# Joint of output projection and feed-forward: a fetch ahead of a large store, weight sums ahead of an input sum, the last rows' steps moved up

## The chip, the cores and the metric

One core of a Trainium2 chip runs the whole program in one launch. The metric is device time in microseconds (us). TensorE (PE) multiplies matrices, VectorE (DVE), ScalarE (ACT) and GpSimd (POOL) work element by element, and SyncE (SP) issues every DMA of this kernel. Each engine takes its instructions in the order in which they were built; waits between engines go over semaphores.

## The reference

One layer of a hybrid decoder on 2048 prompt tokens and 64 sample tokens, 1024 wide, in float32. After attention and gated linear attention, which this change leaves alone, the layer ends so:

```python
mix = jnp.einsum('bte,ed->btd', jnp.concatenate([attn.astype(x.dtype), gla_out], axis=-1), w_out)
x = x + rms_norm(mix, g_mix_post)

h = rms_norm(x, g_ffn_pre)
u = jax.nn.relu(jnp.einsum('btd,df->btf', h, w_up))     # w_up (1024, 4096)
f = jnp.einsum('btf,fd->btd', u * u, w_down)            # w_down (4096, 1024)
x = x + rms_norm(f, g_ffn_post)
```

## The kernel before

**Numbers.** An operand is split into a high and a low part (ACT copies the rounded high part, DVE subtracts it to get the low part), and a product of two operands is three passes on PE. `split_by` makes one such split, `split_in_place` does it for a tile that holds the raw values in the place of its low part.

**Stages.** The rows are worked off in tiles of 128 tokens, 16 of the prompt and one (number 16) of the samples. The output projection takes them in the order `B_ORDER`, which ends with 14, 11, 15. Behind each projection, `residual(i, ...)` does the row work: squares and their sums on ACT, the power -0.5 on POOL, the normalization and the residual sum on DVE (tiles `x1`, `bx`), a second normalization, transposes on PE (`xnT`), and copies into a tile `ht`. The feed-forward then works on two blocks of 1024 tokens (`sb` 0 and 1) and 16 slices of 256 features (`fc`), with a seven-product scheme in place of eight: the input is needed as seven combinations `H[1]` to `H[7]`, the weights as `w` (quarters), `s13` and `s24` (sums of quarters, made in a tile `t13` and split). Four subtractions turn the four quarters in `ht` into the seven combinations, which are stored to `h_d` in DRAM (1,792 KB for each pair of row tiles) and fetched back as `hraw_*`, or, for `H[3]` and `H[4]`, into the place of their low part. `residual` is a generator: each `next(last_rows)` in the code runs the last row tile (15) up to the next `yield`.

**The joint.** While PE does the first slice (`fc` = 0 of `sb` = 0), the last row tiles are finished between its products. The products come in the order `UP_FIRST` = 1, 0, 2, 8, 5, 7, 9, 6, 3, 4; 1 to 7 are products of twelve matmuls, 0, 8 and 9 are steps for the sample tokens (`sam`). `opening(p, ...)` lists what the other engines do behind each. Products 1 and 2 go to the same PSUM bank `ub`: product 1's result is copied out first (`st<-ub` on ACT), then product 2 is added on top of it in the bank. So PE's product 2 waits for that copy. In the trace, products 1 and 2 write `ub`, 5 and 3 write `uc`, 7 and 4 `ud`, 6 `ua`; the next slice begins with `ua` (product 1), `uc` (product 5) and `ue` (product 7).

**Order.** `te`, `ac` and `dv` are PE, ACT and DVE with their instructions held in the order of the code; most instructions of the joint (line L129) are issued so. Other instructions are placed by a scheduler, which also decides when memory of a released pool is taken up again. A tile put where another was waits for the last reader of the other. The output of the up stage is stored slice by slice (`s_d`), and the down stage begins by fetching its first operands (`rs` from `s_d`, `rt` from `t_d`), splitting them into `o0s`, `o1s`, `o0t`, `o1t` and multiplying (`dn`).

Of the kernel before, what the change touches and what calls it, by code (L numbers as in the profile page):

```python
# [16 lines left out]
ALU = mybir.AluOpType  # L17
# [33 lines left out]
DOWN_ORDER = (6, 1, 5, 3, 2, 7, 4)  # L51
DOWN_SUMS = (3, 5, 7, 9, 11, 13)
H_FETCH = ((6, 6), (1, 0), (1, 8), (5, 0), (5, 8), (3, 0), (3, 8))
H_EARLY, H_LATE = (1, 2), (5, 7, 6, 4, 3)
G_EARLY, G_LATE = (0, 1), (2, 3)
A_FILL = ((11, 2, 0), (10, 0, 2), (10, 0, 0), (12, 1, 0))
A_LEAD, A_SPLIT = 14, (2, 1, 0, 0)
# [82 lines left out]
def hybrid_step_kernel(ctx: ExitStack, tc: tile.TileContext, I, O):  # L140
    nc = tc.nc
# [1219 lines left out]
    early = []  # L1361
# [68 lines left out]
    def residual(i, banks, tensor=nc.tensor, scalar=nc.scalar, vector=nc.vector):  # L1430

        n = rows(i)
        x = res_x.pop(i, None) or load_x(i)[0]
        ssq = sp.tile([P, 48], F32, tag="ssq", name=f"bssq_{i}", bufs=2)
        junk = sp.tile([P, D], mybir.dt.bfloat16, tag="junk", name=f"bjunk_{i}", bufs=1)
        x1 = R["x"].tile([P, D], F32, tag="x1", name=f"x1_{i}", bufs=2)
        if i == NB:
            banks = [folded(x1[:NS, c * 512 : (c + 1) * 512], p_) for c, p_ in enumerate(banks)]
        if banks:
            yield from mixed(i, banks, x, x1, junk, ssq, gpost, sp, scalar, vector)  # L1440
        rs = ssq[:, 3:5]
        scalar.activation(junk[:n], x[:n], AF.Square, accum_out=ssq[:n, 2:3])
        yield
        rsqrt_mean(sp, rs[:n, 1:2], ssq[:n, 2:3], n, D, vector=vector)
        vector.scalar_tensor_tensor(x1[:n], x[:n], rs[:n, 1:2], gpre[:n], op0=ALU.mult, op1=ALU.mult)
        yield
        sb, j, second = i // 8, i % 4, i % 8 >= 4
        q = slice(j * P, (j + 1) * P)
        if i < NB and not second and i:
            sums[sb, j] = ht_place(f"ht_{i}")  # L1450
        for h in range(2):
            kk = slice(h * 4, h * 4 + 4)
            pt = (bank([P, 512], "ce"[h], f"xnT_{i}_{h}") if te is tensor else next_bank("cdce", f"xnT_{i}_{h}")).rearrange("p (k t) -> p k t", k=4)
            for k in range(4):
                tensor.transpose(pt[:, k, :n], x1[:n, (h * 4 + k) * P : (h * 4 + k + 1) * P], ident[:n, :n])
            if i == NB:
                split_copy(xsT[:, kk, :NS], xsT[:, kk, NS:], pt[:, :, :NS], vector)
                continue
            ht = sums[sb, j]
            scalar.activation(ht[:, (6, 2)[h] if second else h], pt, AF.Copy)  # L1460
            if sb == 0 and not second:
                split_copy(H[h + 1][0][:, :, q], H[h + 1][1][:, :, q], pt, vector)
        if i == NB or not second:
            return
        yield
        for out, a, b in ((4, 6, 0), (6, 2, 6), (5, 2, 4), (3, 1, 5)):
            vector.tensor_tensor(ht[:, out], ht[:, a], ht[:, b], op=ALU.subtract)
        kept = slice(2 * (sb == 0), 7)
        nc.sync.dma_start(h_d[sb][:, kept, :, q], ht[:, kept])

    h_raws = {}

    def fetch_h(sb, p, home="h"):
        h_raws[p] = []
        for k in range(0, KT // 2, 2):
            if isinstance(home, tuple):
                pool, tag = U[home[k // 2]], "s"
            else:
                pool, tag = {"h": hs_pool, "t": keep}.get(home) or U[home], f"{home}{k // 2}"
            raw = pool.tile([P, 2, BT], F32, tag=tag, name=f"hraw_{sb}_{p}_{k}", bufs=1)  # L1480
            nc.sync.dma_start(raw, h_d[sb][:, p - 1, k : k + 2])
            h_raws[p].append(raw)

    def load_h(sb, p, scalar=nc.scalar, vector=nc.vector):
        h_place(sb, p)
# [38 lines left out]
    for n, i in enumerate(B_ORDER[2:]):  # L1524
        early.append((i, []))
        mixing = out_projecting(nc.tensor, i, early[-1][1])
        run(mixing, 24 if i == B_ORDER[-1] else 48)
        if n == 0:
            second = residual(*early.pop(1))
            next(second)  # L1530
            next(second)
        elif n == 1:
            run(second)
        if n != 1:
            run(residual(*early.pop(0)))
        run(mixing)
        if n == len(B_ORDER) - 5:
            load_up(0, 0)
            split_up(0, 0, 0)
            split_up(0, 0, 1)  # L1540
            fetch_h(0, 5)
# [6 lines left out]
        h_pools[p] = open_pool(f"h_{p}", "right")  # L1548
    U["tmp"] = open_pool("u0_tmp", "right")
    fetch_h(0, 7, ("s24h", "s24l"))  # L1550
    fetch_h(0, 6, "tmp")


    def quarters(sb, fc):
# [9 lines left out]
    def sums_24(sb, fc, vector):  # L1564

        (a11, a21), (a12, a22) = quarters(sb, fc)
        t = sums[sb, fc]
        vector.tensor_tensor(t[:, :, 0], t[:, :, 0], a11, op=ALU.subtract)
        vector.tensor_tensor(t[:, :, 1], a12, t[:, :, 0], op=ALU.subtract)

    def split_sums(sb, fc, n, scalar, vector):
        halves_[sb, fc, n] = parts = [
            U[f"s{n}{'hl'[u]}"].tile([P, KT // 2, 2, P], F32R, tag="s", name=f"s{n}{u}_{sb}_{fc}", bufs=1) for u in range(2)
        ]
        split_by(scalar, vector, *parts, sums[sb, fc])
# [150 lines left out]
    def opening(p, taken, ahead):  # L1726

        if p == 1:
            taken(p)
        elif p == 0:  # L1730
            next(last_rows)
        elif p == 2:
            taken(p)
            next(last_rows)
            run(load_h(0, 6, ac, dv))
            U.pop("tmp").release()
        elif p == 8:
            taken(p)
            sums_24(0, 0, dv)
            split_sums(0, 0, 24, ac, dv)  # L1740
        elif p == 5:
            taken(p)
        elif p == 7:
            taken(p)
            next(last_rows)
            close_pools(R)
            for q in H_LATE[3:]:
                h_pools[q] = open_pool(f"h_{q}")
            for q in H_LATE[:2:-1]:
                h_place(0, q)  # L1750
                for k in range(0, KT // 2, 2):
                    loaded = nc.sync.dma_start(f32(H[q][1][:, k : k + 2]), h_d[0][:, q - 1, k : k + 2])
            with tc.issue_after(loaded.ins):
                load_up(0, 2)
        elif p == 9:
            taken(p)
        elif p == 6:
            split_in_place(3)
            ahead("a")
            taken(p)  # L1760
            split_in_place(4)
            run(last_rows)
            for half in range(2):
                load_down(0, half)
        elif p == 3:
            ahead("s13")
            ahead("13")
        else:
            ahead("s24")
            ahead("24")  # L1770
# [268 lines left out]
    sums_13(0, 0, dv)  # L2039
    run(load_h(0, 5, ac, dv))  # L2040
    split_sums(0, 0, 13, ac, dv)
    load_up(0, 1)
    next(last_rows)
    run(load_h(0, 7, ac, dv))
    for sb in range(NSB):
# [11 lines left out]
            run(ends)  # L2057
        deque(end, 0)
        if sb == 0:
            for p in (3, 4, 7, 6):  # L2060
                h_pools.pop(p).release()
        close_pools(U)
        if sb == 0:
# [53 lines left out]
```

## Time and profile before

| | |
|---|---|
| median of 3 runs | 2221.18 us (2219.98 to 2222.38) |
| profiled execution, own time | 2222.0 us |
| its span, first to last instruction | 2220.2 us |
| mean granted clock of PE in it | 0.996 |
| busy, share of the span | PE 98%, PEld 84%, DVE 68%, ACT 55%, POOL 12% |
| share of the 16 DMA engines (hardware queue) | 55.7% |
| last projection matmuls of row tile 15 | about 901.5 us from the span's start |
| first slice of the up stage on PE | 902.25 to 933.84 us |
| start of the down stage of block 0 | 1258.00 us |

A timeline row has the start in us, the length in us, the engine, the source line, the operation, output<-input, shapes and count; in brackets stands how long the engine was idle before it, and what ended that. Rows that follow each other in one group are merged. In a row of the windows view stand, for each engine, the busy time and the number of instructions in that stretch, then PE's granted clock, the share of the DMA engines and GB/s. Matmul ends are modelled and overlap the next start.

### The profile page before, as it was taken

Reading aid. Unit: us, or ns where it says so; the run is one execution under the profiler, and the core shown is the slowest. Engines: PE = TensorE matmul, PEld = TensorE weight load, DVE = VectorE, ACT = ScalarE, POOL = GpSimd, SP = SyncE. Lnnn points to the kernel's source line nnn. Section 1 sums busy time; section 2 is a strip of 40 time slices with the busy share of each in tenths; the row PEclk is TensorE's granted clock in tenths of the full one; section 3 lists DMA queues with packets and bytes.
Section 4 is the critical chain, followed back from the end, with each engine's and each line's share of the span. In section 5 each row is a group of like instructions: output and inputs, shape, how many; then the busy total and the mean of one; then the engine's idle time right before and its main releaser. Section 6 shows DMA issues by size and latency. Waiting matters only on the chain.

```text
span 2220.2 us, 34144 instructions
## 1 busy us (share of the span) xinstructions
PE 2172.9 (98%) x11784; PEld 1863.6 (84%) x11784; DVE 1518.6 (68%) x3101; ACT 1218.7 (55%) x2626; POOL 261.7 (12%) x417
## 2 busy tenths in 40 slices
PE   8999999999999999899999999999999999999998
PEld 7889888999998888688888887888888888888886
DVE  5888777777876665788888655547776666555566
ACT  6788866556664443555555554435454545444444
POOL 3566522111111100000000000000000000000000
PEclk9999999999999999999999999999999999999999
DMA  7344322214436665867877677767553444666685
GB/s 236 121 137 146 104 90 84 67 58 132 152 110 230 205 194 192 256 218 256 277 272 244 242 238 233 235 192 259 186 186 140 148 157 147 227 199 196 194 267 188
DMA packets 240010, 411.53 MB, mean 185 GB/s; under 512 B 25877, under 2 KB 142077, under 8 KB 235725
## 3 DMA queue, kind: packets, MB, share of 16 engines
q1 hardware_dynamic: 239836, 409.35, 55.7%
q8 instruction: 93, 1.52, 0.3%
q14 instruction: 81, 0.66, 0.1%
HBM read 266.34 MB, written 143.98 MB: 185 GB/s over the span
## 4 chain that ended last, share of the span: by engine, by line
PE 77%; DVE 9%; ACT 8%; DMA 3%; issue 2%; POOL 1%; SPq 0%; DVEq 0%; ACTq 0%; POOLq 0%
PE dn L129 25%; PE gproj L129 9%; PE uc L129 7%; PE ua L129 7%; PE out L1269 6%; PE ud L129 4%; PE ub L129 4%; PE ue L129 4%; ACT s L129 2%; PE proj L129 2%; PE sam L129 1%; PE dsam L129 1%; DVE s L129 1%; PE o L129 1%; PE xT L129 1%
## 5 line engine op out<-in xcount | busy, mean ns | idle before, releaser
L129 PE MATMUL dn<-o0t,o0s 128*128 128x512 f32 x896 | 349.3, 390 | 2.4 <-ACT f L1891 1.1
L129 PE MATMUL dn<-o1t,o0s 128*128 128x512 f32 x896 | 349.5, 390 | 0.5 <-DVE o1t L217 0.5
L129 PE MATMUL dn<-o0t,o1s 128*128 128x512 f32 x896 | 349.3, 390 | 0.0
L217 DVE TENSOR_TENSOR o1s<-rs,o0s 128x512 fp32r<-128x512 f32 x224 | 154.8, 691 | 231.2 <-ACT o0s L216 228.4
L216 ACT ACTIVATE o0s<-rs 128x512 fp32r<-128x512 f32 x224 | 141.1, 631 | 305.8 <-PE dn L129 283.8
L129 PE MATMUL gproj<-wg,gx 128*128 128x384 f32 x1408 | 264.7, 342 | 2.9 <-ACT dec L1025 1.8
L129 PEld LDWEIGHTS gproj<-wg,gx 128*128 128x128 f32 x1408 | 241.0, 188 | 7.8 <-issue 3.9
L129 ACT ACTIVATE st<-st 128x512 f32<-128x512 f32 x224 | 141.2, 630 | 141.9 <-DVE st L129 137.9
L129 PEld LDWEIGHTS dn<-o0t,o0s 128*128 128x128 f32 x896 | 168.2, 188 | 39.9 <-ACT f L1891 1.5
L129 PEld LDWEIGHTS dn<-o1t,o0s 128*128 128x128 f32 x896 | 168.2, 188 | 37.4 <-DVE o1t L217 1.4
L129 PEld LDWEIGHTS dn<-o0t,o1s 128*128 128x128 f32 x896 | 168.2, 188 | 35.2
L129 PE MATMUL uc<-H,s 128*128 128x512 f32 x768 | 187.7, 393 | 1.7 <-ACT s L129 1.2
L129 PE MATMUL ua<-H,w 128*128 128x512 f32 x744 | 179.2, 390 | 0.0
L129 PEld LDWEIGHTS uc<-H,s 128*128 128x128 f32 x768 | 143.6, 189 | 33.2 <-ACT s L129 1.6
L129 PEld LDWEIGHTS ua<-H,w 128*128 128x128 f32 x744 | 139.7, 188 | 29.4
L1269 PE MATMUL out<-wo,mt 128*128 128x512 f32 x680 | 158.6, 392 | 0.0
L217 DVE TENSOR_TENSOR o1t<-rt,o0t 128x512 fp32r<-128x512 f32 x224 | 153.5, 685 | 7.5 <-ACT o0t L216 7.3
L206 POOL TENSOR_TENSOR frs<-rs_v,half 128x1 f32<-128x1 f32 (+1 forms) x13 | 10.1, 787 | 1214.7 <-DVE rs_v L204 693.5
L1269 PEld LDWEIGHTS out<-wo,mt 128*128 128x128 f32 x680 | 126.5, 188 | 26.1
L216 ACT ACTIVATE o0t<-rt 128x512 fp32r<-128x512 f32 x224 | 138.2, 617 | 8.5 <-DMA rt<-t_d 8.2
L129 DVE TENSOR_TENSOR st<-st 128x512 f32<-128x512 f32 x160 | 110.6, 691 | 26.6 <-ACT st L129 22.3
L129 ACT ACTIVATE s<-t 128x1024 fp32r<-128x1024 f32 x62 | 65.7, 1060 | 96.8 <-PE ua L129 27.9
(393 smaller groups left out, 4224.8 us busy)
## 6 DMA issues: line engine op xcount, KB each, us to landing
s_d<-st SPq DMA_DIRECT2D x32, 1792.0 KB, 9.8
rs<-s_d SPq DMA_DIRECT2D x224, 256.0 KB, 2.9
raw<-in_w_up SPq DMA_DIRECT2D x64, 512.0 KB, 4.6
rt<-t_d SPq DMA_DIRECT2D x128, 256.0 KB, 4.4
rt<-in_w_down SPq DMA_DIRECT2D x96, 256.0 KB, 3.2
t<-in_w_down SPq DMA_DIRECT2D x64, 256.0 KB, 4.1
t_d<-t SPq DMA_DIRECT2D x32, 512.0 KB, 3.4
gx<-xt_d SPq DMA_DIRECT2D x28, 512.0 KB, 6.0
```

The lines of the kernel that those rows point to most:

```text
L129: ins = call(*a, **k)
L206: nc.gpsimd.tensor_tensor(out, v[:n], e, op=ALU.pow)
L216: nc.scalar.activation(hi, src, AF.Copy)
L217: vector.tensor_tensor(lo, src, f32(hi), op=ALU.subtract)
L1269: te.matmul(banks[c], x, w[:, c * 512 : (c + 1) * 512], start=k + u == 0, stop=k == KT - 1 and u == len(products) - 1,)
```

## The change

- The store of row tiles 10 and 14 to `h_d` is held back by one `yield`, until both fetches of `H[6]` have been issued; the load of the second slice of `w_up` now comes behind that store as well.
- For row tile 15, the residual sum and the second square are now issued before the splits of `H[7]` and before product 1's copy; the second normalization goes behind sample step 0, and the transposes behind product 5 instead of product 7.
- The weight sums `s24` (`sums_24`) go behind step 0 and their split ahead of the splits of `H[6]`.
- The four subtractions of the last `ht` go from DVE to POOL.
- `H[3]` and `H[4]` swap their places in memory and their order of loading; the loads come behind product 5 and no longer behind product 7, and with them the loads of a third slice of `w_up` and of the first pieces of `w_down`. `H[3]`'s split comes behind step 9, ahead of the split of the next `w`.

```diff
--- before.py
+++ after.py
@@ -51,7 +51,7 @@
 DOWN_ORDER = (6, 1, 5, 3, 2, 7, 4)
 DOWN_SUMS = (3, 5, 7, 9, 11, 13)
 H_FETCH = ((6, 6), (1, 0), (1, 8), (5, 0), (5, 8), (3, 0), (3, 8))
-H_EARLY, H_LATE = (1, 2), (5, 7, 6, 4, 3)
+H_EARLY, H_LATE = (1, 2), (5, 7, 6, 3, 4)
 G_EARLY, G_LATE = (0, 1), (2, 3)
 A_FILL = ((11, 2, 0), (10, 0, 2), (10, 0, 0), (12, 1, 0))
 A_LEAD, A_SPLIT = 14, (2, 1, 0, 0)
@@ -1463,9 +1463,12 @@
         if i == NB or not second:
             return
         yield
+        adder = vector if tensor is nc.tensor else nc.gpsimd
         for out, a, b in ((4, 6, 0), (6, 2, 6), (5, 2, 4), (3, 1, 5)):
-            vector.tensor_tensor(ht[:, out], ht[:, a], ht[:, b], op=ALU.subtract)
+            adder.tensor_tensor(ht[:, out], ht[:, a], ht[:, b], op=ALU.subtract)
         kept = slice(2 * (sb == 0), 7)
+        if i == B_ORDER[-3]:
+            yield
         nc.sync.dma_start(h_d[sb][:, kept, :, q], ht[:, kept])
 
     h_raws = {}
@@ -1478,8 +1481,9 @@
             else:
                 pool, tag = {"h": hs_pool, "t": keep}.get(home) or U[home], f"{home}{k // 2}"
             raw = pool.tile([P, 2, BT], F32, tag=tag, name=f"hraw_{sb}_{p}_{k}", bufs=1)
-            nc.sync.dma_start(raw, h_d[sb][:, p - 1, k : k + 2])
+            fetched = nc.sync.dma_start(raw, h_d[sb][:, p - 1, k : k + 2])
             h_raws[p].append(raw)
+        return fetched
 
     def load_h(sb, p, scalar=nc.scalar, vector=nc.vector):
         h_place(sb, p)
@@ -1531,7 +1535,10 @@
             next(second)
         elif n == 1:
             run(second)
-        if n != 1:
+        if i == B_ORDER[-1]:
+            waiting_rows = residual(*early.pop(0))
+            run(waiting_rows, 5)
+        elif n != 1:
             run(residual(*early.pop(0)))
         run(mixing)
         if n == len(B_ORDER) - 5:
@@ -1548,7 +1555,9 @@
         h_pools[p] = open_pool(f"h_{p}", "right")
     U["tmp"] = open_pool("u0_tmp", "right")
     fetch_h(0, 7, ("s24h", "s24l"))
-    fetch_h(0, 6, "tmp")
+    sixth = fetch_h(0, 6, "tmp").ins
+    with tc.issue_after(sixth):
+        run(waiting_rows)
 
 
     def quarters(sb, fc):
@@ -1729,39 +1738,38 @@
             taken(p)
         elif p == 0:
             next(last_rows)
+            sums_24(0, 0, dv)
         elif p == 2:
             taken(p)
-            next(last_rows)
+            split_sums(0, 0, 24, ac, dv)
             run(load_h(0, 6, ac, dv))
             U.pop("tmp").release()
         elif p == 8:
             taken(p)
-            sums_24(0, 0, dv)
-            split_sums(0, 0, 24, ac, dv)
         elif p == 5:
-            taken(p)
-        elif p == 7:
             taken(p)
             next(last_rows)
             close_pools(R)
             for q in H_LATE[3:]:
                 h_pools[q] = open_pool(f"h_{q}")
-            for q in H_LATE[:2:-1]:
+            for q in H_LATE[3:]:
                 h_place(0, q)
                 for k in range(0, KT // 2, 2):
                     loaded = nc.sync.dma_start(f32(H[q][1][:, k : k + 2]), h_d[0][:, q - 1, k : k + 2])
             with tc.issue_after(loaded.ins):
                 load_up(0, 2)
+                for half in range(2):
+                    load_down(0, half)
+        elif p == 7:
+            taken(p)
         elif p == 9:
             taken(p)
+            split_in_place(3)
         elif p == 6:
-            split_in_place(3)
             ahead("a")
             taken(p)
             split_in_place(4)
             run(last_rows)
-            for half in range(2):
-                load_down(0, half)
         elif p == 3:
             ahead("s13")
             ahead("13")
@@ -2039,7 +2047,9 @@
     sums_13(0, 0, dv)
     run(load_h(0, 5, ac, dv))
     split_sums(0, 0, 13, ac, dv)
-    load_up(0, 1)
+    with tc.issue_after(sixth):
+        load_up(0, 1)
+    next(last_rows)
     next(last_rows)
     run(load_h(0, 7, ac, dv))
     for sb in range(NSB):
@@ -2057,7 +2067,7 @@
             run(ends)
         deque(end, 0)
         if sb == 0:
-            for p in (3, 4, 7, 6):
+            for p in (4, 3, 7, 6):
                 h_pools.pop(p).release()
         close_pools(U)
         if sb == 0:
```

On ACT, at the start of the feed-forward, from the squares of row tile 15 on. `H70` is the high part of `H[7]`, `st_0_0<-ub_0_0` the copy of product 1 and then of product 2, `bjunk_15<-bx_15` the second square of row tile 15. Before:

```order
L129 ACTIVATE bjunk_15_10977,bssq_15_10976<-out_15_1_10798 128x512
L129 ACTIVATE H70_0_10985<-hraw_0_7_0_10949 128x1024
L129 ACTIVATE H70_0_10985<-hraw_0_7_2_10951 128x1024
L129 ACTIVATE st_0_0_11008<-ub_0_0_10991 128x512
L129 ACTIVATE bjunk_15_10977,bssq_15_10976<-bx_15_10974 128x1024
L129 ACTIVATE st_0_0_11008<-ub_0_0_10991 128x512
```

The same place now:

```order
L129 ACTIVATE bjunk_15_10977,bssq_15_10976<-out_15_1_10798 128x512
L129 ACTIVATE bjunk_15_10977,bssq_15_10976<-bx_15_10974 128x1024
L129 ACTIVATE H70_0_10990<-hraw_0_7_0_10948 128x1024
L129 ACTIVATE H70_0_10990<-hraw_0_7_2_10950 128x1024
L129 ACTIVATE st_0_0_11013<-ub_0_0_10996 128x512 x2
L1460 ACTIVATE ht_11_10900<-xnT_11_0_10901 128x512
```

The second square has moved ahead of `H70` and of product 1's copy.

On DVE, from the first sum with `ud` on: `H31` and `H41` are the low parts of `H[3]` and `H[4]`, `w01_0_1` a low part of the next weights, `ht_11` the last row tiles' quarters. Before:

```order
L129 TENSOR_TENSOR H31_0_11111<-H31_0_11111,H30_0_11110 128x1024 x2
L129 TENSOR_TENSOR w01_0_1_11141<-raw0_0_1_10970,w00_0_1_11140 128x1024
L129 TENSOR_TENSOR st_0_0_11008<-st_0_0_11008,ua_0_0_10993 128x512
L129 TENSOR_TENSOR st_0_0_11008<-st_0_0_11008 128x512
L129 TENSOR_TENSOR H41_0_11115<-H41_0_11115,H40_0_11114 128x1024 x2
L129 TENSOR_TENSOR ht_11_10901<-ht_11_10901 128x512 x4
L129 TENSOR_TENSOR st_0_0_11008<-st_0_0_11008,uc_0_0_10992 128x512
```

The same place now:

```order
L129 TENSOR_TENSOR H31_0_11098<-H31_0_11098,H30_0_11097 128x1024 x2
L129 TENSOR_TENSOR w01_0_1_11147<-raw0_0_1_10970,w00_0_1_11146 128x1024
L129 TENSOR_TENSOR st_0_0_11013<-st_0_0_11013,ua_0_0_10998 128x512
L129 TENSOR_TENSOR st_0_0_11013<-st_0_0_11013 128x512
L129 TENSOR_TENSOR H41_0_11102<-H41_0_11102,H40_0_11101 128x1024 x2
L129 TENSOR_TENSOR st_0_0_11013<-st_0_0_11013,uc_0_0_10997 128x512
```

The four `ht_11` subtractions have left DVE; they stand on POOL, behind its power for row tile 15, and wait for ACT's copies of `xnT_15`.

On ACT, where the up stage of block 0 ends and the down stage begins. `o0s` and `o0t` are high parts of down operands; the places of `H[3]` and `H[4]`, which `o0t` takes over, have been swapped. Before:

```order
L216 ACTIVATE o0s_0_6_0_13986<-rs_0_6_0_13974 128x512
L216 ACTIVATE o0t_0_6_0_13990<-rt_0_6_0_13976 128x512
L216 ACTIVATE o0s_0_6_1_13994<-rs_0_6_1_13978 128x512
L129 ACTIVATE st_0_15_13783<-st_0_15_13783 128x512
L216 ACTIVATE o0t_0_6_1_13998<-rt_0_6_1_13980 128x512
```

The same place now:

```order
L216 ACTIVATE o0s_0_6_1_13994<-rs_0_6_1_13978 128x512
L129 ACTIVATE st_0_15_13783<-st_0_15_13783 128x512
L216 ACTIVATE o0s_0_6_2_14010<-rs_0_6_2_13982 128x512
L129 ACTIVATE st_0_15_13783<-st_0_15_13783 128x512
L129 ACTIVATE st_0_15_13783<-ua_0_15_13757 128x512
L129 ACTIVATE st_0_15_13783<-st_0_15_13783 128x512
L129 ACTIVATE samq_15_13891<-sam_15_13761 128x128
L216 ACTIVATE o0t_0_6_0_13990<-rt_0_6_0_13976 128x512
L216 ACTIVATE o0t_0_6_1_13998<-rt_0_6_1_13980 128x512
```

The first `o0t` has moved behind the steps of the last slice: it now takes the place of `H[4]`, whose last reader is product 4, the last of the up stage, and no longer that of `H[3]`, whose last reader is product 3.

## The prediction

> **What bounds the kernel now.** I read the page first, then PE's timeline over the joint, then the chain of waits there, and last ACT, DVE and POOL in the same microseconds. The page says where time can come from:
>
> ```profile
> PE 2172.9 (98%) x11784; PEld 1863.6 (84%) x11784; DVE 1518.6 (68%) x3101; ACT 1218.7 (55%) x2626; POOL 261.7 (12%) x417
> PE 77%; DVE 9%; ACT 8%; DMA 3%; issue 2%; POOL 1%; SPq 0%; DVEq 0%; ACTq 0%; POOLq 0%
> ```
>
> PE is the bound nearly everywhere, and no matmul is added or taken away. So the change is worth what it does to the holes in PE's row, and what a hole does to PE's clock. The rows of PE at the joint (in brackets the idle time before a group and what ended it):
>
> ```profile
> 902.25 3.02 PE L129 MATMUL ub<-H,w 128*128 128x512 f32 x12
> 906.06 2.93 PE L129 MATMUL ub<-H,w 128*128 128x512 f32 x12
> 912.53 2.88 PE L129 MATMUL ud<-H,s 128*128 128x512 f32 x12
> 915.25 1.03 PE L129 MATMUL xnT<-ident,x 128*128 128x128 f32 x8
> 916.87 0.44 PE L129 MATMUL sam<-ident,both 128*128 128x128 f32 x2 [0.58 <-ACT both L129]
> 920.28 0.73 PE L129 MATMUL ua<-H,s 128*128 128x512 f32 x2 [2.96 <-ACT s L129]
> 921.54 4.63 PE L129 MATMUL ua<-H,s 128*128 128x512 f32 x10 [0.53 <-DVE s L129]
> 925.97 3.75 PE L129 MATMUL uc<-H,s 128*128 128x512 f32 x12
> 931.21 2.79 PE L129 MATMUL ud<-H,w 128*128 128x512 f32 x11 [0.76 <-DVE H L129]
> 933.84 2.88 PE L129 MATMUL ua<-H,w 128*128 128x512 f32 x12
> 937.90 0.73 PE L129 MATMUL uc<-H,s 128*128 128x512 f32 x2 [1.18 <-ACT s L129]
> 941.56 2.88 PE L129 MATMUL ue<-H,s 128*128 128x512 f32 x12
> ```
>
> Up to 916.87 PE runs without a hole worth the name. The first is the 2.96 us before product 6, the last the 1.18 and 0.53 us inside the next slice. What set the time between is in the chain of waits:
>
> ```profile
> 918.20 4.61 DMA H<-h_d
> 922.83 1.06 ACT H L129
> 925.07 1.22 DVE w L129
> 928.86 1.05 ACT H L129
> 931.08 1.22 DVE H L129
> ```
>
> The load that ends last of the first of `H[3]` and `H[4]` runs from 918.2 to 922.8, and from there ACT and DVE work through the splits of `H[3]`, of the next weights, the sums and `H[4]`. Product 4's second matmul, at 931.21, ends the chain. So the yardstick is: the landing of the load, plus 931.21 - 922.83 = 8.4 us.
>
> **A new hole before product 2.** Product 2 adds onto a bank from which ACT must first copy product 1. On ACT stood, and now stands in another order:
>
> ```profile
> 902.25 2.00 ACT L129 ACTIVATE H<-hraw 128x1024 fp32r<-128x1024 f32 x2
> 905.30 0.60 ACT L129 ACTIVATE st<-ub 128x512 f32<-128x512 f32 x1 [1.06 <-PE ub L129]
> 909.05 1.06 ACT L129 ACTIVATE bjunk<-bx 128x1024 bf16<-128x1024 f32 x1 [3.15 <-DVE bx L129]
> ```
>
> The copy came the moment product 1 was done. Now the square (third row) is queued ahead of both the two splits of `H[7]` and the copy, and it waits for the residual sum on DVE, which waits for a power on POOL:
>
> ```profile
> 903.91 0.15 DVE L129 TENSOR_SCALAR rs_v<-bssq 128x1 f32<-128x1 f32 x1
> 906.30 1.40 DVE L129 SCALAR_TENSOR_TENSOR x<-out,bssq,gpost 128x512 f32<-128x512 f32 x2
> 907.74 1.22 DVE L129 TENSOR_TENSOR bx<-x,bx 128x1024 f32<-128x1024 f32 x1
> 910.47 0.54 POOL L206 TENSOR_TENSOR bssq<-rs_v,half 128x1 f32<-128x1 f32 x1 [4.82 <-DVE rs_v L129]
> ```
>
> Worked through: the variance is ready at 904.06, POOL's power takes 0.54 and the passing on 0.1 to 0.2 (the last row begins 0.08 us after its input ends), so 904.75; the normalization 1.40 and the sum 1.22 bring DVE to 907.45; the square starts at 907.5 and takes 1.06, the two splits 2.00: 910.55. The copy takes 0.60: PE starts product 2 at about 911.2 instead of 906.06. That is a hole of **5.1 us** where none was. Behind ACT's waiting square stand only these, but PE stands behind them, and nothing else in PE's order can fill the time.
>
> **What of it reaches the end.** Product 2, sample step 8 and product 5 take 912.53 - 906.06 = 6.47 us, so PE is at 917.7. The transposes of row tile 15 now follow there (1.03 us): 918.7. By then their input has long been normalized (the square ends near 908.6, and one power on POOL and one normalization on DVE have nine us). The loads into the place of `H[3]` wait for these transposes, since the memory that is closed there holds row tile 15. Their second half is issued about 0.36 us after the first, near 919.1. How long they take:
>
> ```profile
> raw<-in_w_up SPq DMA_DIRECT2D x1, 512.0 KB, 3.9
> ```
>
> That is a transfer of the same size alone; the one at 918.20 took 4.61 among others. Between the two I take 4.1: landing at 923.2 against 922.81, **+0.4**. Product 4's second matmul would come at 931.6.
>
> **What goes at the end.** From 933.84 to 941.56 PE spends 7.72 us on two products which take 2.72 each elsewhere (915.25 - 912.53): 2.3 us of holes. They came from DVE, which worked off four subtractions before the weight sums that the second of those products needs:
>
> ```profile
> 932.21 2.74 DVE L129 TENSOR_TENSOR ht<-ht 128x512 f32<-128x512 f32 x4
> ```
>
> With the subtractions on POOL the holes go: **-2.3**. Next late there is nothing within 2 us. Together with the +0.4 the plain shift is **-1.9**.
>
> **The clock.** A hole costs more than its length. The windows view (PE, PEld, DVE, ACT, POOL busy with counts, then PE's granted clock) over the old hole, over what followed it, and over one window at half clock earlier in the run:
>
> ```profile
> 917.30:920.30 3.00, 0.04 (x2) 0.03 (x1) 1.84 (x4) 1.13 (x2) 0.00 (x0) 1.00 0.79 219
> 920.30:927.70 7.40, 6.87 (x17) 5.08 (x18) 6.67 (x7) 4.41 (x7) 0.00 (x0) 0.54 1.02 377
> 36.91:40.32 3.41, 3.41 (x13) 3.41 (x13) 2.12 (x7) 0.91 (x4) 3.03 (x6) 0.50 0.51 166
> ```
>
> After 3 us of idle PE ran for 7.4 us at 0.54. Today that spell is free, because the chain over `H[3]` ends later anyway. Now there are two long holes, and both spells lie on the path. The one behind product 2 delays the transposes, hence the loads, hence everything behind. The other comes where PE, done with product 6 early, waits for the splits of `H[3]` and `H[4]` (over 3 us, since the yardstick fixes when product 4 can go on), and its slow spell falls on product 4 and the next slice. One window of 3.41 us at 0.50 loses 1.7 us, the longer spell 7.40 x 0.46 = 3.4. I take 2.3 for each, nearer to the short one because small holes and the position in the window cut some of it: **+4.6**.
>
> The Trainium skill, page "TensorE: Matmul & The Clock Gate", section "What's actually happening", has the clock return to full after one busy window of about 3.4 us; by that each spell would cost at most 1.7 us and the sum below would be 1.2 lower, +4.7. The spell of 7.40 us at 0.54 here lasted longer than one such window, so the trace speaks against it.
>
> **POOL's subtractions beside DVE.** They wait for ACT's copies of `xnT_15`, behind the transposes that end at 918.7, so they begin near 921, just when DVE makes the low parts of `H[3]` and of the next weights. How such neighbours get on is shown by an earlier place, where POOL and DVE both read SBUF with two inputs:
>
> ```profile
> 348.91 1.28 POOL L972 TENSOR_TENSOR sg<-sg,ggla 128x512 f32<-128x512 f32 x1
> 349.20 1.14 DVE L1028 TENSOR_TENSOR after<-after,before 128x128 f32<-128x128 f32 x1
> 351.27 0.27 DVE L1028 TENSOR_TENSOR after<-after,before 128x128 f32<-128x128 f32 x1
> ```
>
> The DVE operation beside POOL's took 1.14 us, and ended when POOL's did; alone it took 0.27. So a DVE operation waits for POOL's. Four on POOL of 1.28 us make 5.1 us in which three DVE operations of the chain want in. If the two alternate, two waits of 1.28 and a bit come on top, 2.7; if DVE is served back to back, 0.3. I take **+2.7**, since the row shows the full wait, not a shared one.
>
> The Trainium skill, page "SBUF — State Buffer", section "SBUF: two separate sides", describes a port pair that GpSimd and VectorE share and that one holds for a whole instruction; the 1.14 against 0.27 agrees.
>
> **The start of the down stage.** The first `o0t` now takes the place of `H[4]`, whose reader is the last product of the stage:
>
> ```profile
> 1258.00 0.39 PE L129 MATMUL dn<-o0t,o0s 128*128 128x512 f32 x1
> 1260.09 0.50 PE L129 MATMUL dn<-o0t,o0s 128*128 128x512 f32 x1 [0.56 <-DVE samq L129]
> 1252.84 0.62 ACT L216 ACTIVATE o0t<-rt 128x512 fp32r<-128x512 f32 x1
> 1253.68 0.69 DVE L217 TENSOR_TENSOR o1t<-rt,o0t 128x512 fp32r<-128x512 f32 x1
> ```
>
> It was split 5 us ahead. Now ACT can begin when PE is through, about 1258.2; 0.62 later the first matmul can go, 0.69 after that (1259.5) the first with a low part, and the second pair is one DVE operation behind, 1260.2. Two matmuls and the small hole lead to 1260.6 where 1260.09 stood: **+0.5**.
>
> **What I cost at nothing.** `H[6]` was fetched behind the store and bounded product 6's hole; it is now fetched first, but the loads of `H[3]` end later than product 6 does in either case, so the gain is covered. If it weren't, it would be at most the 2.96 us of the old hole. The second slice of `w_up` comes behind the store, and ACT needs it for the weights behind the first split of `H[3]`, at about 923.2 + 1.06 = 924.3; its loads of 3.9 us stand on SP ahead of those of `H[3]`, which are issued at 918.7. If they came late, each us would count in full. The `s24` sums and their splits move to times where DVE and ACT waited (3.15 us before the square alone). The first `w_down` pieces queue on SP behind the loads of `H[3]` and wait for memory; behind them stand stores whose readers are in the down stage.
>
> **The sum.** -1.9 + 2.3 + 2.3 + 2.7 + 0.5 = **+5.9 us**. The profiled execution takes 2222.0 us by its own time (span 2220.2), 0.8 above the median of 2221.2; so 2227.9 there, and against the median **2227.1 us**. A difference of 0.2%, 4.4 us, is about what a measurement of this kernel can tell from no change.
>
> **Rivals.** *No change that can be told.* DVE gets its three splits in back to back (0.3 for 2.7), and each slow spell is a single window (1.7 for 2.3): -1.9 + 1.7 + 1.7 + 0.3 + 0.5 = +2.3, 2223.5 us. For it: the half-clock window at 36.91 lasted 3.41 us. Against: the spell at 920.30, and the full wait at 349.20. Mixed cases lie near the bound of 4.4, on both sides. Chance 0.28.
>
> *Faster.* Product 1's copy comes in time after all. It decides itself at the square: if the residual sum were on DVE early enough for the square to start by 902, ahead of the splits, ACT would reach the copy by 905.3. Then PE runs through, the transposes end at 906.06 + 6.47 + 1.03 = 913.6, and the loads could land 0.4 + 4.1 later, at 918.1; with the store and the weights on the queue then I take 919.8, 3.0 us before today's 922.8; without the first spell, with the end's 2.3 saved and 0.5 lost, and most of the second spell hidden, that gives -3.0 - 2.3 + 0.5 = -4.8, 2216.4 us. For it: today ACT stands idle 3.15 us before that square. Against: the variance is only ready at 904.06, so three operations and POOL must come between. Chance 0.05.
>
> *The change doesn't do what it says*: the early loads of `H[3]` gain nothing, because the transposes that free their memory come later by the new hole. That is part of my forecast (+0.4 instead of the 3 us earlier that the order allows).
>
> **How the numbers follow.** Forecast, slower by over 0.2%: 0.67; within: 0.28; faster: 0.05. The range from its terms: at the low end one window at 0.50 (1.7) for the one spell, 1.4 for the other, 0.3 for POOL, 0.5 for the down stage: -1.9 + 1.7 + 1.4 + 0.3 + 0.5 = +2.0; at the high end two spells of 3.4, 2.8 for POOL, 0.7 for the down stage: -1.9 + 6.8 + 2.8 + 0.7 = +8.4. To hold the cases with a small first hole too I take the low end one lower, +1.0: 2222.2 to 2229.6.
>
> **What would show it right or wrong.** Right: in PE's timeline an idle of about 5 us before the second group of `ub`, ended by ACT's `st`; the granted clock near 0.5 behind it; transposes of `xnT` directly behind the first `uc`; no hole before the `uc` of the next slice; DVE's `H` rows behind the loads stretched beyond 1.22 us while POOL shows `ht`; the first `dn` some 0.8 us behind the last up product. Wrong: a copy `st<-ub` that starts with the end of product 1 (then the time falls); full clock right after the hole, or unstretched `H` rows on DVE (then it is the no-change case); a load of `H[3]` that lands well before 922 although the transposes are late, which would mean that its memory isn't what it waited for.

## The result and the profile after

The changed kernel takes 2225.98 us (median of 21 runs, 2223.95 to 2228.49) against 2222.17 us (21 runs, 2219.34 to 2225.15) for the kernel before: ratio 1.0016, 95% interval 1.001 to 1.0023, so 2.2 to 5.1 us slower (3.8 by the medians). A second comparison on another occasion gave 1.0017 (1.0007 to 1.0026). The forecast was 2227.1 us, 5.9 us slower; the sign and the range held, the size was too large, and the median lies in the case "within 0.2%" that had a chance of 0.28.

The profiled execution has a span of 2224.7 us, 4.5 above that of before. PE at the joint, timeline rows of the changed kernel:

```profile
903.31 3.02 PE L129 MATMUL ub<-H,w 128*128 128x512 f32 x12
912.20 4.51 PE L129 MATMUL ub<-H,w 128*128 128x512 f32 x12 [4.92 <-ACT st L129]
920.26 1.03 PE L129 MATMUL xnT<-ident,x 128*128 128x128 f32 x8
928.23 1.67 PE L129 MATMUL uc<-H,s 128*128 128x512 f32 x6 [0.94 <-DVE H L129]
930.45 1.43 PE L129 MATMUL uc<-H,s 128*128 128x512 f32 x5 [0.56 <-DVE H L129]
935.18 0.49 PE L129 MATMUL ud<-H,w 128*128 128x512 f32 x1 [3.30 <-ACT H L129]
936.44 4.12 PE L129 MATMUL ud<-H,w 128*128 128x512 f32 x11 [0.77 <-DVE H L129]
945.85 2.88 PE L129 MATMUL ue<-H,s 128*128 128x512 f32 x12
959.60 0.44 PE L129 MATMUL sam<-ident,both 128*128 128x128 f32 x2 [0.73 <-ACT both L129]
959.79 2.98 PE L129 MATMUL ue<-H,w 128*128 128x512 f32 x12
```

The new hole stands in the second row: 4.92 us, ended by ACT's copy `st`. The hole before product 6 is gone, one of 3.30 us before product 4 has come, and the holes before `uc` in the next slice have gone. ACT ahead of the first hole, in the new order (square, two splits, copy):

```profile
908.62 1.06 ACT L129 ACTIVATE bjunk<-bx 128x1024 bf16<-128x1024 f32 x1 [5.22 <-DVE bx L129]
909.68 1.98 ACT L129 ACTIVATE H<-hraw 128x1024 fp32r<-128x1024 f32 x2
911.57 0.57 ACT L129 ACTIVATE st<-ub 128x512 f32<-128x512 f32 x1
```

The windows view (us, five engines, PE's granted clock, DMA share, GB/s) over the half-clock spell of product 2 and a stretch behind it, then over that of product 4:

```profile
912.01:915.42 3.41, 3.22 (x8) 2.55 (x9) 2.75 (x4) 0.13 (x1) 0.54 (x1) 0.50 0.93 229
915.61:919.02 3.41, 3.41 (x20) 2.96 (x19) 0.80 (x2) 2.28 (x5) 0.00 (x0) 1.00 0.72 275
935.90:939.32 3.42, 2.88 (x7) 2.30 (x8) 3.42 (x5) 0.17 (x1) 0.00 (x0) 0.50 1.15 347
```

Each time the clock is at 0.50 for 3.4 us and then full again. In the kernel before, the same view over 920.94 to 927.77 shows 0.50 for 6.83 us; the 7.40 us at 0.54 of the prediction is this spell with a margin. Where POOL meets DVE (timeline rows of both):

```profile
922.99 6.33 POOL L1468 TENSOR_TENSOR ht<-ht 128x512 f32<-128x512 f32 x4 [9.20 <-ACT ht L129]
926.49 3.91 DVE L129 TENSOR_TENSOR H<-H,H 128x1024 fp32r<-128x1024 f32 x2 [1.62 <-ACT H L129]
```

The two low splits of `H[3]` took 3.91 us instead of 2.45, and POOL's four subtractions 6.33. Next, the end of the up stage, where `dn` waits for its first operands:

```profile
1257.79 2.99 PE L129 MATMUL ue<-H,w 128*128 128x512 f32 x12
1261.50 0.51 PE L129 MATMUL dn<-o0t,o0s 128*128 128x512 f32 x1 [0.72 <-ACT o0t L216]
1262.23 0.51 PE L129 MATMUL dn<-o1t,o0s 128*128 128x512 f32 x1 [0.22 <-DVE o1t L217]
```

For comparing kernels I cut PE's row at the same instructions in each profile: product 1's start (902.25 before, 903.31 after), product 4's second matmul (931.21, 936.44), the first `ue` of the next slice (941.56, 945.85), its second `ue` group (957.15, 959.79), and the thirteenth `dn` of the down stage (1261.58, 1264.87). All numbers are us between such starts, worked out before rounding, so that the last digit can be one off; "again" is a second profile of the same kernel.

| kernel | product 1 to 4 | to the first `ue` | to the second `ue` | sum | to `dn` 13 |
|---|---|---|---|---|---|
| before | 28.96 | 10.35 | 15.58 | 54.90 | 304.44 |
| before, again | 29.37 | 10.35 | 15.60 | 55.31 | 304.08 |
| after | 33.13 | 9.41 | 13.94 | 56.48 | 305.08 |
| after, again | 33.51 | 9.59 | 13.75 | 56.85 | 305.06 |
| square_back | 28.07 | 10.95 | 13.00 | 52.01 | 305.11 |
| subs_dve | 31.95 | 10.43 | 15.56 | 57.94 | 305.05 |
| places_back | 33.90 | 9.40 | 13.94 | 57.25 | 304.08 |
| fetch_only | 27.67 | 10.37 | 15.57 | 53.61 | 304.10 |
| filled_hole | 31.14 | 10.60 | 12.99 | 54.74 | 306.02 |
| square_subs | 27.89 | 10.74 | 15.26 | 53.88 | 305.07 |
| sq_four | 25.76 | 8.59 | 15.59 | 49.93 | 305.08 |
| sq_four_places | 23.50 | 9.93 | 15.59 | 49.02 | 304.09 |

The change costs +4.2 up to product 4, gives back 0.9 and 1.6 behind it, and loses 0.6 to 1.0 at the down stage: about +2.4 in the pairs of profiles. Of the rest of the 4.5 us between the two spans, the 1.1 before product 1 isn't the change's (the two profiles of the changed kernel differ by 2.5 us there). The 1.2 behind `dn` 13 is half in the second profile; what of it belongs to the change is open, see the last two runs.

### The profile page after: what moved, and what is told of

Read it like the earlier page. It is cut to its first block, busy times and chain, and to the rows that moved or that the text cites. A ratio compares the mean times of both kernels' runs of the same rounds, so it can differ in the third digit from the quotient of the medians.

```text
span 2224.7 us, 34149 instructions
## 1 busy us (share of the span) xinstructions
PE 2173.4 (98%) x11784; PEld 1865.6 (84%) x11784; DVE 1516.3 (68%) x3097; ACT 1218.3 (55%) x2626; POOL 266.6 (12%) x421
## 4 chain that ended last, share of the span: by engine, by line
PE 79%; ACT 8%; DVE 8%; DMA 2%; issue 2%; POOL 1%; SPq 0%; DVEq 0%; ACTq 0%; POOLq 0%
PE dn L129 26%; PE gproj L129 9%; PE uc L129 8%; PE ua L129 7%; PE out L1269 6%; PE ub L129 4%; PE ud L129 4%; PE ue L129 4%; ACT s L129 2%; PE proj L129 2%; PE sam L129 1%; PE dsam L129 1%; PE o L129 1%; DVE s L129 1%; PE xT L129 1%
```

## The experiments

Each was timed in five rounds against the kernel before; the ratios are to that.

**square_back.** In the changed kernel, the second `next(last_rows)` goes back from the stage's start to behind product 2:

```diff
     next(last_rows)
-    next(last_rows)
     run(load_h(0, 7, ac, dv))
...
         elif p == 2:
             taken(p)
+            next(last_rows)
             split_sums(0, 0, 24, ac, dv)
```

(so the square is issued with the `next` behind product 1's copy; a line keeps `H[4]`'s loads behind `H[3]`'s, here and in all kernels below that build on this or put the places back.)

> The changed kernel with the residual sum and the second square of row tile 15 behind product 1's copy again; all else as changed. Theory (the copy that waits behind the square makes the first hole): no hole of 4.9 us before product 2, full clock there, transposes of row tile 15 about 6.5 us earlier; the loads of H[3] land 3 to 5 us earlier; the next slice then gives back about 1.6 us of it, since in the kernel before ACT and DVE were late there. Total 2 to 4 us below the changed kernel, so within 1.5 us of the kernel before. Rival (the loads of H[3] are bound by other transfers, the hole is covered): within 0.7 us of the changed kernel.

Measured: 2219.24 us, ratio 0.999 (0.9981 to 0.9999): 0.2 to 4.2 us below the kernel before, and 6.7 below the changed one by medians. PE's rows:

```profile
904.51 2.92 PE L129 MATMUL ub<-H,w 128*128 128x512 f32 x12
912.22 1.15 PE L129 MATMUL xnT<-ident,x 128*128 128x128 f32 x8 [1.09 <-ACT ht L1460]
927.51 0.50 PE L129 MATMUL ud<-H,w 128*128 128x512 f32 x1 [3.06 <-ACT H L129]
928.77 5.06 PE L129 MATMUL ud<-H,w 128*128 128x512 f32 x11 [0.76 <-DVE H L129]
933.63 3.50 PE L129 MATMUL ua<-H,w 128*128 128x512 f32 x12
```

No hole before product 2, full clock there, and 5.1 us less up to product 4: the splits of `H[3]` come 3.6 us earlier behind product 1's start, and the way from them to product 4 is 1.5 us shorter. So the copy queued behind the square is the cause of the loss at the joint. POOL was done before the splits began here:

```profile
914.93 5.25 POOL L1468 TENSOR_TENSOR ht<-ht 128x512 f32<-128x512 f32 x4 [5.47 <-ACT ht L129]
920.35 2.38 DVE L129 TENSOR_TENSOR H<-H,H 128x1024 fp32r<-128x1024 f32 x2 [3.40 <-ACT H L129]
```

The expected giving back in the next slice didn't come: its 13.00 us are even less than the changed kernel's 13.94. So what the next slice gained in the changed kernel was not owed to the late PE, as the expectation had it. square_back saved more than the 2 to 4 us expected; its profile shows 4.5 to 4.8 of the 6.7 at the joint, and where the rest lies is open.

**filled_hole.** Useless matmuls ahead of product 2:

```diff
+            if first and p == 2:
+                hi, lo = H[5]
+                for n in range(18):
+                    k = n // 3 % 4
+                    te.matmul(Z, weight(sb, fc, 5, n % 3 // 2, k), (hi, lo, hi)[n % 3][:, k], start=n in (0, 9), ...)
             if 0 < p < 8:
```

> The changed kernel with 18 matmuls of no use (product 5's operands, into product 5's own bank, which product 5 then starts anew) in PE's order ahead of product 2, about 4.1 us of work in the hole of 4.9 us. Theory (idle time halves the clock): product 2 runs at full clock, 2.9 us in place of 4.5, the loads of H[3] and all behind them come 1.6 us earlier; the time falls by about 1.6 us against the changed kernel. Rival (product 2 is slowed by the DMA traffic or by its operands, not by the hole): product 2 takes 4.5 us still, no gain.

Measured: 2222.04 us, ratio 1.0003 (0.9994 to 1.0012): with 18 more matmuls the kernel is faster than without, by 2.9 us by the ratios and 3.9 by the medians, though the two intervals just overlap. PE, and the windows view over product 2:

```profile
904.11 4.27 PE L129 MATMUL uc<-H,s 128*128 128x512 f32 x18
909.19 3.04 PE L129 MATMUL ub<-H,w 128*128 128x512 f32 x12 [0.81 <-ACT st L129]
```

```profile
909.19:912.06 2.87, 2.87 (x12) 2.36 (x13) 2.21 (x4) 1.09 (x2) 0.54 (x1) 1.00 0.96 270
```

With 0.96 of the DMA engines busy, against 0.93 in the changed kernel, product 2 takes 3.04 instead of 4.51: it was the idle time, not the traffic or the operands, that set the clock. The path gains 2.0 us up to product 4: 1.4 in the landing, the rest since POOL, 2.2 us earlier behind product 1's start, meets the splits less. Up to the second `ue` 1.7 to 2.1 us are left of that, near the 1.6 expected. At the down stage this profile loses 0.9 us (306.02 in the table) in a hole of 1.15 us before the second `dn`, ended by DVE's `o1t`; what makes the times gain more than the joint is open.

**subs_dve.** The subtractions on DVE, the other parts as changed:

```diff
-        adder = vector if tensor is nc.tensor else nc.gpsimd
+        adder = vector
```

> The changed kernel with the four subtractions of row tile 15 on DVE again. Theory (POOL's subtractions hold up the splits by 2.7 us): the two low splits of H[3] take 2.45 us again in place of 3.9, product 4's second matmul comes 2.7 us earlier after the landing (8.4 in place of 11.05); in the next slice the holes before the weight sums come back (2.3 us). Total 0.4 us below the changed kernel (from -1.5 to +0.5). Rival (POOL's work beside DVE costs nothing on the path): 2.3 us above the changed kernel, from the holes that come back.

Measured: 2225.72 us, ratio 1.0016 (1.0007 to 1.0026), within 0.3 us of the changed kernel. DVE, and PE in the next slice:

```profile
925.38 2.45 DVE L129 TENSOR_TENSOR H<-H,H 128x1024 fp32r<-128x1024 f32 x2 [1.55 <-ACT H L129]
934.87 2.74 DVE L129 TENSOR_TENSOR ht<-ht 128x512 f32<-128x512 f32 x4
```

```profile
933.87 5.06 PE L129 MATMUL ud<-H,w 128*128 128x512 f32 x11 [0.47 <-DVE H L129]
959.66 0.44 PE L129 MATMUL sam<-ident,both 128*128 128x128 f32 x2 [1.65 <-ACT both L129]
```

The split is back at 2.45, but product 4 comes only 1.2 us earlier: 1.5 from the splits, less 0.3 for a later landing. From there it takes 10.43 to the first `ue`, because product 4 ran slowly. A fast one would have won next to nothing: DVE's split of the sums for the second product behind it ends at 941.81, 7.94 us behind product 4's second matmul, and in the kernel before, where PE waits for that split, it is 7.90 in both profiles (10.35 in both, though product 4 took 2.79 in one and 4.36 in the other). And the next slice takes 15.56 again. So POOL's part was: 1.5 lost at the splits, 1.0 won at the end of the first slice, 1.6 in the next. By these cuts subs_dve is 1.1 to 1.5 us slower than the changed kernel, where 0.4 us faster was expected; the times don't tell the two apart.

**square_subs.** square_back and subs_dve together.

> As square_back, but with the four subtractions on DVE, so only the fetch, the order of the weight sums and the earlier transposes are left of the change. Theory (what POOL gains lies in the next slice as much as in this): product 4's second matmul no later than in square_back, since POOL's subtractions were done there before the splits began; the holes before the sums of the next slice (2.3 us) and before its sample step (1.7 us, and small ones) come back, the slow clock behind product 4 hides in them: 1.5 to 3 us above square_back, about 2221 to 2222 us. Rival (the subtractions only cost where they meet the splits): equal to square_back.

Measured: 2223.98 us, ratio 1.0008 (0.9999 to 1.0017). By the profile the next slice takes 15.26, 2.3 more than in square_back, as the theory has it; the times say 4 to 5 us more, of which I can't place the rest. The direction is clear, the size is not.

**places_back.** The places of `H[3]` and `H[4]`, and the release, as before:

```diff
-H_EARLY, H_LATE = (1, 2), (5, 7, 6, 3, 4)
+H_EARLY, H_LATE = (1, 2), (5, 7, 6, 4, 3)
...
-            for p in (4, 3, 7, 6):
+            for p in (3, 4, 7, 6):
```

> The changed kernel with the places of H[3] and H[4] as before (the order of their loads stays: H[3] first). Theory: the first o0t of the down stage is split ahead again, the first dn follows the last up product without a hole, 0.5 to 0.9 us are saved, nothing else moves. Rival (the wait for the sample step covers it): no difference from the changed kernel at the seventh dn matmul.

Measured: 2224.78 us, ratio 1.0014 (1.0005 to 1.0023). The up stage runs into the down stage without a hole:

```profile
1258.62 2.99 PE L129 MATMUL ue<-H,w 128*128 128x512 f32 x12
1261.45 0.39 PE L129 MATMUL dn<-o0t,o0s 128*128 128x512 f32 x1
1261.68 0.40 PE L129 MATMUL dn<-o1t,o0s 128*128 128x512 f32 x1
```

The stretch to `dn` 13 is 304.08 against 305.08: 1.0 us, and it separates every kernel of the table by where its places lie (304.1 or 304.4 against 305.05 and more). At the joint product 4 came 0.8 later, against the "nothing else moves". The queue on SP, in places_back and in the changed kernel:

```profile
923.74 1.76 SPq L1759 DMA_DIRECT2D H<-h_d  x4
921.32 2.81 SPq L1758 DMA_DIRECT2D H<-h_d  x4
```

`H[3]` is loaded first in both, and in the kernel before too: the change swaps the places and not the order of loading. What each load waits for changes with the places. In the changed kernel `H[3]`'s loads go out when the transposes of row tile 15 end (921.29), and `H[4]`'s when the last low part of `H[6]` does (923.31). In places_back `H[3]`'s loads wait for that low part (923.71), 2.0 us behind the transposes. Behind product 1's start this is 2.4 us later; in sq_four_places against sq_four it is 1.5 us later (14.19 against 12.69). So this much is the places' doing. What becomes of it is not: product 4 came only 0.8 us later here, since POOL was done as the splits began (928.82 and 928.77), and 2.3 us earlier in sq_four_places, where the loads took less long and no slow spell came.

**fetch_only.** The kernel before with this part of the change alone:

```diff
+        if i == B_ORDER[-3]:
+            yield
...
+        if i == B_ORDER[-1]:
+            waiting_rows = residual(*early.pop(0))
+            run(waiting_rows, 5)
...
+    sixth = fetch_h(0, 6, "tmp").ins
+    with tc.issue_after(sixth):
+        run(waiting_rows)
...
+    with tc.issue_after(sixth):
+        load_up(0, 1)
```

> The kernel before with only the fetch of H[6] ahead of the store (and w_up's second slice behind it). Theory: H[6] lands several us earlier, the hole of 2.96 us before product 6 shrinks or goes; the loads of H[3] now wait for the transposes of row tile 15, issued 1 to 1.5 us earlier; the end of the joint stays bound by them: 0 to 1.5 us below the kernel before. Rival (H[6] bounded the joint all the way): 3 us below. Rival (the delayed store and w_up hold up the next slice): slower by over 1 us.

Measured: 2220.11 us, ratio 0.9996 (0.9987 to 1.0004): not told apart from no change. The rows of PE, and of DVE and the queue on SP where the loads of `H[3]` go out:

```profile
918.64 0.73 PE L129 MATMUL ua<-H,s 128*128 128x512 f32 x2 [0.66 <-ACT s L129]
930.15 0.79 PE L129 MATMUL ud<-H,w 128*128 128x512 f32 x1 [3.28 <-ACT H L129]
931.41 4.97 PE L129 MATMUL ud<-H,w 128*128 128x512 f32 x11 [0.47 <-DVE H L129]
```

```profile
913.81 2.36 DVE L129 TENSOR_TENSOR H<-hraw,H 128x1024 fp32r<-128x1024 f32 x2
916.20 2.39 SPq L1760 DMA_DIRECT2D H<-h_d  x4
```

The hole before product 6 shrank from 2.96 to 0.66 us, and 1.3 us came through to product 4; the rest has moved to the hole before product 4. In one point the theory was wrong: the loads of `H[3]` still waited for the low part of `H[6]` (it ends at 916.17), as in the kernel before (917.81), not for the transposes. They went out 3.1 us earlier behind product 1's start than before (916.20 - 903.74 against 917.84 - 902.25), and lost most of it on the way.

**sq_four.** square_back with the split of `H[4]` ahead of the next weights and of the sums behind product 6:

```diff
         elif p == 6:
+            split_in_place(4)
             ahead("a")
             taken(p)
-            split_in_place(4)
             run(last_rows)
```

> As square_back, with the split of H[4] right behind that of H[3], ahead of the split of the next weights and of the sums behind product 6. Theory (H[4]'s split waits on ACT behind squares that wait for DVE's sums; the hole of 3 us before product 4 and the slow clock behind it come from this order alone): the hole goes, product 4 runs at full clock; some of it comes back as a wait for the weight sums in the next slice. 1 to 4.5 us below square_back, 2.5 likeliest, so near 2216.7 us. Rival (the loads of H[4] land too late): the hole stays, ended by a DMA, same time as square_back.

Measured: 2217.75 us, ratio 0.9982 (0.9973 to 0.9991). The hole before product 4 went, and 4.7 us up to the first `ue`; 2.6 of it came back in the next slice (15.59 against 13.00), so 2.1 are left. Other than expected, product 4 was not at full clock; product 3 and it shared a spell of 3.42 us at 0.50 (926.42 to 929.84):

```profile
928.93 3.37 PE L129 MATMUL ud<-H,w 128*128 128x512 f32 x12
```

**sq_four_places.** sq_four with places_back.

> As sq_four, with the places of H[3] and H[4] as in the kernel before. Theory: the start of the down stage loses its hole again, 0.5 to 1.1 us below sq_four, nothing else. Rival: the places set when the loads of H[3] can start (the tile of row 15 lies in one of them), so the joint moves by more than 1 us.

Measured: 2215.53 us, ratio 0.9973 (0.9963 to 0.9982), 2.7‰ or some 6 us below the kernel before and the fastest here. PE's rows:

```profile
922.28 2.82 PE L129 MATMUL uc<-H,s 128*128 128x512 f32 x11 [0.85 <-DVE H L129]
924.94 2.90 PE L129 MATMUL ud<-H,w 128*128 128x512 f32 x12
950.49 0.44 PE L129 MATMUL sam<-ident,both 128*128 128x128 f32 x2 [1.66 <-ACT both L129]
```

Product 4 follows product 3 without a hole and at full clock. So the hole of 3 us before product 4 came from where its split stood in the order of ACT and DVE. The next slice's 1.66 us are back: what was gained meets the same ACT and DVE work earlier, as sq_four's expectation allowed.

**after_again** and **before_again** are the two kernels a second time.

> The changed kernel once more, for a second profile. Theory (what lies outside the joint and the start of the down stage varies from execution to execution): from product 1's start to the next slice's ue product 56.5 us again, within 0.8; the 0.7 us that the first profile lost at the end of the down stage of block 0, and the 1.1 us before the joint, are not there again or differ. Time 2224 to 2226 us. Rival (the change reaches past the joint): the same 0.7 us at the same place, against the second profile of the kernel before.

> The kernel before once more, for a second profile: 54.9 us from product 1's start to the next slice's ue product, within 0.8, the hole of 2.96 us before product 6 again, the half-clock spell behind it again; time 2221 to 2223 us. If the joint differs by more than 1 us between the two profiles, single profiles can't carry the terms of the sum.

Measured: 2225.47 and 2221.17 us; the table has their cuts. Product 4 in the one and in the other:

```profile
934.34 4.30 PE L129 MATMUL ud<-H,w 128*128 128x512 f32 x11 [0.77 <-DVE H L129]
```

```profile
929.91 4.36 PE L129 MATMUL ud<-H,w 128*128 128x512 f32 x11 [0.76 <-DVE H L129]
```

The sums of either kernel repeat within 0.4 us, so terms of half a us can be read from these cuts. The speed of one product doesn't repeat so well: in before_again the spell behind the hole before product 6 began inside the hole (0.50 from 917.12 to 923.95), and a second one of 3.42 us met product 4. Outside it, one term did repeat against my expectation: the hole where the down stage of block 0 ends. The first row is of before_again, the second of after_again:

```profile
1554.02 0.50 PE L129 MATMUL dn<-o0t,o0s 128*128 128x512 f32 x1 [0.78 <-DVE f L1819]
```

```profile
1557.67 0.50 PE L129 MATMUL dn<-o0t,o0s 128*128 128x512 f32 x1 [1.39 <-DVE f L1827]
```

In the first profiles it is 0.46 and 1.29 us. So it may be the change's 0.6 to 0.8 us; but in the other kernels it lies between 0.40 (subs_dve) and 1.42 (square_subs) without regard to which part of the change they hold. This stays open.

## Why the prediction was right in sign and too large

- **The hole before product 2:** forecast 5.1 us, measured 4.92, with the named cause and at the named place. square_back takes it away.
- **The loads of `H[3]`:** from product 1's start to the second of their splits it was 20.58 us before (922.83 - 902.25; 21.01 in the second profile) and is 23.3 now in both. That is +2.7 or +2.3, where the +0.4 and the +2.3 for the first slow spell stood. That the sum fits is partly luck, since two sizes were off in opposite directions: the spell cost 1.6 and 2.0 (product 2 took 4.51 and 4.88, against 2.92; in the second profile its spell began inside the hole and ran from 906.91 to 913.73), and from the issue of the second half to its split it took 4.9 and 4.6 us, where the prediction took 4.1 for the transfer.
- **POOL beside DVE:** forecast 2.7, measured 1.45 and 1.8 (from that split to product 4's second matmul, 9.83 and 10.2 against 8.38). The rows of single operations show why, DVE's two splits of `H[3]` and the last two of POOL's four:

```profile
926.49 1.68 DVE L129 TENSOR_TENSOR H<-H,H 128x1024 fp32r<-128x1024 f32 x1 [1.62 <-ACT H L129]
928.10 2.30 DVE L129 TENSOR_TENSOR H<-H,H 128x1024 fp32r<-128x1024 f32 x1
925.79 1.29 POOL L1468 TENSOR_TENSOR ht<-ht 128x512 f32<-128x512 f32 x1
927.16 2.15 POOL L1468 TENSOR_TENSOR ht<-ht 128x512 f32<-128x512 f32 x1
```

  They alternate, as the prediction had it: DVE's first split waits 0.46 us for the end of POOL's third operation (1.68 against 1.22), POOL's fourth waits 0.86 for that split, and DVE's second waits 1.08 for POOL's fourth (in the second profile the two splits wait 0.77 and 1.09). The step that failed is "two waits of 1.28 and a bit": when the splits began, POOL had worked for 3.5 us, so one wait was only the rest of an operation, and the split of the next weights met none. The prediction's own times had this in them (an estimate): with POOL from 921 and the first low split at 923.2 + 1.06 = 924.3, POOL's third operation has 0.5 to 0.6 us to go, and 1.28 more gives 1.8 to 1.9. The rule of the Trainium skill's page "SBUF — State Buffer", section "SBUF: two separate sides", one engine holding the shared port pair for a whole instruction, agrees with these rows.
- **The second slow spell:** forecast 2.3, measured 1.3 and 1.5 (4.12 and 4.30 against 2.79). The row of 7.4 us at 0.54 misled: it was a spell of 6.83 us, and product 4's was one of 3.42. But in square_back product 4 and the product behind it lose 2.3 + 0.6 us, in a spell as long as the one of before. The first row is of before, the second of square_back:

```profile
920.94:927.77 6.83, 6.30 (x16) 4.88 (x16) 6.03 (x7) 3.84 (x6) 0.00 (x0) 0.50 1.01 371
928.02:934.84 6.82, 6.07 (x14) 4.80 (x15) 5.57 (x8) 2.59 (x4) 0.00 (x0) 0.50 0.81 244
```

  So both lengths occur, and the hole ahead doesn't tell which: it was 3.30 us in the changed kernel and 3.06 in square_back. What decides it is open. The Trainium skill's page "TensorE: Matmul & The Clock Gate", section "What's actually happening", has the full clock back after one busy window of about 3.4 us. Product 4's spell in the changed kernel agrees with that; the one in square_back, with PE busy for 6.07 us of it, doesn't.
- **The next slice:** this is the term that was missing. I wrote "Next late there is nothing within 2 us", and let the subtractions' gain end with the first slice. In the kernel before, the next slice loses 1.68 us before its sample step and some 0.7 in small holes around it:

```profile
956.96 0.44 PE L129 MATMUL sam<-ident,both 128*128 128x128 f32 x2 [1.68 <-ACT both L129]
```

  Without the subtractions on DVE the next slice takes 13.94 instead of 15.58: -1.6, and subs_dve and square_subs, which put them back, lose it again. So it is the backlog of ACT and DVE; in sq_four it is back at 15.59 with the subtractions on POOL, where PE comes to the next slice 4.7 us earlier.
- **The first slice's end:** the 2.3 us went as forecast; 9.41 against 10.35 is -2.3 with the spell's 1.3.
- **The down stage:** forecast +0.5, measured +0.6 to +1.0.

With the measured terms: +2.7 + 1.5 - 2.3 + 1.3 - 1.6 + 0.8 = +2.4, within the times' 2.2 to 5.1 though at its lower end; with the open 0.6 to 0.8 at the end of the down stage it would be about 3. So the forecast of 5.9 had the named hole and its consequences, and was too large by the next slice's 1.6, by POOL's 0.9 to 1.2 and by the second spell's 0.8 to 1.0.

## What to carry to other kernels

An instruction moved up on an in-order engine is paid by whoever waits for the one it has passed: look for what it waits for itself, and what the engine's next result releases. An operation taken off a loaded engine can be worth time in a later stage too, not only at the next wait (1.6 us in the next slice here). And a hole in PE's row may be another engine's order: moving one split ahead of sums that weren't urgent won 4.7 us up to the next slice, of which 2.1 were left behind it.

## What the runs showed of the hardware

Work of no use can save time: 18 matmuls in a hole of 4.9 us kept the granted clock at 1.00 for the product behind it, which began at 0.50 without them. In the profiles here every half-clock spell at the joint lasted 3.4 or 6.8 us, also behind holes of the same length of about 3 us (3.42 in the changed kernel, 6.83 in the kernel before, 6.82 in square_back). And DVE and POOL, both with two inputs from SBUF, waited for each other by whole operations: POOL's four subtractions took 6.33 us beside two of DVE's splits, and 5.25 without.
